# Splitting the sparse-attention weights in the first feed-forward layer and keeping both parts in DRAM

## The chip, the cores and the metric

One core of a Trainium2 chip runs the whole program in one launch. The metric is the device time in microseconds (us) of that launch; lower is better. The engines that matter are TensorE (PE, matrix products), VectorE (DVE), ScalarE (ACT), GpSimd (POOL) and the DMA queues that SyncE (SP) and GpSimd issue to. Data lives in DRAM, in SBUF (128 partitions) and in PSUM, into which PE writes.

## The reference, cut to what matters

Two layers over T = 1040 tokens (16 learned ones, then 1024), D = 1024. Layer 0 mixes tokens with gated linear attention (GLA), layer 1 with sparse attention (DSA); a SwiGLU feed-forward layer follows each.

```python
def dsa_mixer(h, w_in, g_kv, w_uk, w_uv, w_out, rel_bias):
    proj = h @ w_in
    q, c, q_idx, k_idx, w_idx = jnp.split(proj, [s1, s2, s3, s4], axis=-1)
    c = rmsnorm(c, g_kv)
...
        s_idx = jnp.einsum('bqhd,bsd->bqhs', qib, k_idx) * IDX_DIM ** -0.5
        score = jnp.einsum('bqhs,bqh->bqs', jax.nn.relu(s_idx), wb)
        top_val, top_idx = lax.top_k(score, n_sel)          # 256 keys of each query
        c_sel = jax.vmap(lambda cb, ib: cb[ib])(c, top_idx)
        q_lat = jnp.einsum('bqhd,hcd->bqhc', qb, w_uk)
        logits = jnp.einsum('bqhc,bqkc->bhqk', q_lat, c_sel) * ATT_HEAD_DIM ** -0.5
        logits = logits + bias                               # T5 relative bias, then softmax
        u = jnp.einsum('bhqk,bqkc->bqhc', p, c_sel)
        return jnp.einsum('bqhc,hcd->bqhd', u, w_uv)
    return o @ w_out

def swiglu(h, w_in, w_out):
    gate, up = jnp.split(h @ w_in, 2, axis=-1)
    return (jax.nn.silu(gate) * up) @ w_out
```

Everything is float32.

## The kernel before

**Arithmetic.** Each float32 operand of a product is split into two parts of the type fp32r, a rounded high part (`wh`, `xh`, ...) and the rest (`wl`, `xl`, ...). `mm3` then makes each product with three matmuls: high by high (L198), high by low (L199) and low by high (L200). So every weight that arrives from DRAM has to be split before PE can use it.

**Weights.** `Weights` holds the list of all weight tiles in their order of use. `get` hands out a tile and, with `ahead`, starts the load of the next one. `load_split` loads a tile of 128 x 2048 (1 MB; 128 x 1024 for some) in two pieces into raw buffers (`wraw`, two of them, SP's queue, L184), makes the high part with a cast (L186 on ACT, or L188 on GpSimd where `whigh` is set) and the low part with a subtraction (L189, on the engine `wlow`). The parts go to a ring of two slots, each a pair `wh`, `wl`. `wlow` is VectorE, except from the index stage to the end of attention, where it is GpSimd; `whigh` is GpSimd during the top-k stage.

**Stages in time.** GLA runs to about 400 us and its output projection to 450. The first feed-forward layer runs from 450 to about 1290: eleven groups of two gate tiles, and in each group per gate tile (`hidden`) three pieces of the token axis (352, 344, 344 columns), with the down projection of the group before in between. Then come the index stage with its scores (`kidx`, `qidx0`, `qidx1`; to about 1381), the top-k stage (to about 1605), attention (to about 1810), the output projection (`do0` to `do3`, to about 1880) and the second feed-forward layer to the end. In the top-k stage the program's text interleaves two kinds of steps: a step-by-step search on VectorE for each query's threshold (L1053 counts with `jd`; L1062 `below`, L1070 `cand`, L1073 and L1076 `flip` move the bounds, on 128 x 3 or 128 x 4 numbers), and the units of latent, queries (`dq0` to `dq3`), keys and values (`ukv0`) on PE with their evictions. Attention splits the other three `ukv` tiles in pieces of 512 columns.

**Order.** Each engine takes its instructions in the program's order, SP and GpSimd also their DMA issues, and each instruction waits for its own inputs and for free buffers. Buffers come from pools: a tile of a name with n buffers waits for the release of the one n before it.

Of the kernel before, what the change touches and what calls it, by code (L numbers as in the profile page):

```python
# [9 lines left out]
F32 = mybir.dt.float32  # L10
F32R = mybir.dt.float32r
# [22 lines left out]
WIDE = [(META, 512), (META + 512, 512)]  # L34
REL = 1
RING, RAW = 2112, 1056
EARLY = 5
GROUPS = (([7, 1, 4, 3], (2, 2)), ([5, 2, 6], (1, 1)))
N1, S2, M2, S3, M3 = 1, 3, 2, 8, 2
# [40 lines left out]
class Weights:  # L80
# [4 lines left out]

    def load(self, i):
        if i < len(self.seq) and self.seq[i] is not None and i not in self.tiles:
            _, src, n = self.seq[i]
            self.tiles[i] = self.k.load_split(src, n)

    def get(self, name, ahead=True):
        i = self.i
# [16 lines left out]
class Trunk:  # L109
    def __init__(self, ctx, tc, io, out):  # L110
        self.tc, self.nc, self.io, self.out = tc, tc.nc, io, out
        nc = self.nc
        self.main = ctx.enter_context(tc.tile_pool(name="main", bufs=1))
        self.ring = ctx.enter_context(tc.tile_pool(name="ring", bufs=2))
        self.rawp = ctx.enter_context(tc.tile_pool(name="raw", bufs=2))
        self.psp = ctx.enter_context(tc.tile_pool(name="ps", bufs=8, space=bass.MemoryType.PSUM))
        m = self.main
        self.later = Later()
        self.wlow = nc.vector
        self.whigh = None  # L120
        self.xh = m.tile([128, KT, T], F32R, name="xh")
        self.xl = m.tile([128, KT, T], F32R, name="xl")

        self.xm = m.tile([128, KT, 48], F32R, name="xm")
        self.h = m.tile([128, KT, T], F32, name="h0", tag="H")

        self.ident = m.tile([128, 128], F32, name="ident")
        self.mean = m.tile([128, 128], F32, name="mean")
        self.sufm = m.tile([128, 128], F32R, name="sufm")
        self.totm = m.tile([128, 2], F32, name="totm")  # L130
        self.gains = m.tile([128, 6, KT], F32, name="gains")
        self.eps = m.tile([128, 1], F32, name="eps")
        nc.vector.memset(self.mean, 1.0 / D)
        nc.vector.memset(self.eps, EPS)
        nc.gpsimd.tensor_scalar_mul(self.xm[:, :, META:32], self.mean.rearrange("p (k c) -> p k c", k=KT), 0.0)

        nc.scalar.activation(m.tile([128, 1], F32, name="root"), self.eps, AF.Sqrt)
        self.sufraw = m.tile([128, 128], F32, name="sufraw")

        seq = [("ka%d" % i, io["w_ka"][i], KT * 264) for i in range(2)]  # L140
        for h in range(4):
            seq += [("gq%d" % h, io["w_gq"][h], 1024), ("gr%d" % h, io["w_gr"][h], 2048),
                    ("gv%d" % h, io["w_gv"][h], 2048)]
        seq += [("go%d" % i, io["w_go"][i], 2048) for i in range(4)]
        seq += self.ffn_seq(0)
        seq += [("kidx", io["w_kidx"], 1024)]
        seq += [("qidx%d" % i, io["w_qidx"][i], 2048) for i in range(2)]
        seq += [("c", io["w_c"], 2048)]
        seq += [("dq%d" % i, io["w_dq"][i], 2048) for i in range(4)]
        seq += [None]  # L150
        seq += [("do%d" % i, io["w_do"][i], 2048) for i in range(4)]
        seq += self.ffn_seq(1)
        self.w = Weights(self, seq)

        dram = lambda name, shape: nc.dram_tensor(name, shape, F32).ap()
        self.s_h = dram("s_h", (128, KT, T))
        self.s_rel = dram("s_rel", (8, NREL))
        self.s_skew = dram("s_skew", (8, 128, NREL))
# [14 lines left out]
    def ps(self, dt=F32):  # L173
        return self.psp.tile([128, 512], dt, name="ps")

    def load_split(self, src, n, pool=None, tags=("wh", "wl"), cap=RING, raw=None, piece=RAW):
        nc = self.nc
        pool = pool or self.ring
        hi = pool.tile([128, cap], F32R, name=tags[0])
        lo = pool.tile([128, cap], F32R, name=tags[1])  # L180
        for a in range(0, n, piece):
            e = min(n, a + piece)
            r = raw() if raw else self.rawp.tile([128, RAW], F32, name="wraw")
            nc.sync.dma_start(r[:, : e - a], src[:, a:e])  # L184
            if self.whigh is None:
                nc.scalar.copy(hi[:, a:e], r[:, : e - a])  # L186
            else:
                self.whigh.tensor_copy(hi[:, a:e], r[:, : e - a])  # L188
            self.wlow.tensor_sub(lo[:, a:e], r[:, : e - a], hi[:, a:e].bitcast(F32))  # L189
        return hi, lo  # L190

    def split(self, hi, lo, src, low=None):
        self.nc.scalar.copy(hi, src)  # L193
# [466 lines left out]
            after(c)  # L660


    def ffn(self, pool, tmp, chunks, last_chunks, squares, after):
        nc, w, later = self.nc, self.w, self.later
        v = nc.vector
        G = NF // 2

        def hidden(hh, hl, wi, q, a, n):
            pg = self.proj_fm(wi, 256, 0, a, n)
            later.tick()  # L670
            pu = self.proj_fm(wi, 256, 128, a, n)
            sg = tmp.tile([128, 512], F32, name="sg")
            t = tmp.tile([128, 512], F32, name="t")
            nc.scalar.activation(sg[:, :n], pg[:, :n], AF.Silu)  # L674
            v.tensor_mul(t[:, :n], sg[:, :n], pu[:, :n])  # L675
            self.split(hh[:, q, a : a + n], hl[:, q, a : a + n], t[:, :n])
            later.tick()
# [17 lines left out]
        for g in range(G):  # L695
# [39 lines left out]
            else:  # L735
                chunks = WIDE if self.layer else chunks
                for q in range(2):
                    wi = w.get("fi%d" % (2 * g + q))
                    for a, n in chunks:
                        hidden(hh, hl, wi, q, a, n)  # L740
                    if q == 0 or g == G - 2:
                        wo = w.get("fo%d" % (g - 1 + q))
                        order = [(d, c) for d in range(KT) for c in chunks]
                        if q:
                            order = [(d, c) for c in chunks for d in range(KT)]
                        for d, (a, n) in order:
                            out(*(prev if q == 0 else (hh, hl)), wo, d, a, n)
                        later.tick()
            prev = (hh, hl)

    def ffn_phase(self, layer, begun, norm_row, last_chunks, after, emit=None, cover=()):

# [2 lines left out]
        with ExitStack() as ctx:  # L755
# [33 lines left out]

            applies = []  # L790
            self.out_end(begun, lambda c: squares(*chunks[c]), normed)
            self.ffn(pool, tmp, chunks, last_chunks, squares, ended)
            for f in cover[:1]:
                f()
            self.later.drain()
# [4 lines left out]
    def index_begin(self):  # L800

        self.begun = {}

        def keys(c):
            a, n = ALL[c]
            self.begun["k", a] = self.proj_fm(self.wk, 128, 0, a, n)

        def first():
            self.wlow = self.nc.gpsimd
            self.wk = self.w.get("kidx")  # L810
            keys(0)

        def rest():
            keys(1)
            self.wq0 = self.w.get("qidx0", ahead=False)
            for e in range(2):
                self.begun["q", 144, e] = self.proj_fm(self.wq0, 256, e * 128, 144, 384)

        return first, rest

    def dsa(self):
# [1 line left out]
        v = nc.vector  # L823
        off = [sum(nkeys(j) for j in range(b)) for b in range(9)]
        with ExitStack() as ctx:
            self.wlow = nc.gpsimd
            self.kv = {}
            dp = ctx.enter_context(tc.tile_pool(name="dsa", bufs=1))
            cth = dp.tile([128, 2, T], F32R, name="cth")
# [75 lines left out]
            with tc.tile_pool(name="topk", bufs=1) as tp, tc.tile_pool(name="cn", bufs=2) as cp:  # L905
                qf = self.main.tile([128, 8, SEQ], F32, name="qf", tag="H")
                steps = self.topk(tp, sc, mask, off)
                costs = [1.7] * 66 + [MASK] * 8
                self.whigh = nc.gpsimd

                def parts(c, j):

                    a, n = FRAMES[c]
# [29 lines left out]
                        done += 1  # L943
                later.drain()
                att.begin(steps, len(costs) - done)
                self.whigh = None
            att.run(ctx, mp)
            h = self.main.tile([128, KT, T], F32, name="h1", tag="H")
            for k in range(KT):
# [224 lines left out]
            v.memset(mask[0:64, off[b + 1] - 64 : off[b + 1]], NEG)  # L1174
            yield

    def keys(self, pool, p, raw=None, piece=RAW):

        kh = self.ring.tile([128, RING], F32R, name="wh")
        kl = self.ring.tile([128, RING], F32R, name="wl")  # L1180
        uh, ul = self.load_split(self.io["w_ukv"][p], 1024, pool, ("uh", "ul"), 1024, raw, piece)
        self.kv[p] = (uh, ul, kh, kl)
        for e in range(2):
            for a, n in ALL:
                q = self.ps()[:, :n]
                for j in range(2):
                    s = slice((e * 2 + j) * 128, (e * 2 + j) * 128 + 128)
                    self.mm3(q, uh[:, s], ul[:, s], self.cth[:, j, a : a + n], self.ctl[:, j, a : a + n],
                             j == 0, j == 1)
                s = slice(e * T + a, e * T + a + n)  # L1190
                self.split(kh[:, s], kl[:, s], q)
# [26 lines left out]
    def attention(self, sp, mask, off, sc):  # L1218
# [128 lines left out]
        def run(ctx, mp):  # L1347
# [7 lines left out]
            for j, (hd, m) in enumerate(units):  # L1355
# [18 lines left out]
                if m == 3 and hd < 6:  # L1374
                    table(hd + 2)
                if m == KEYS_AT and hd % 2 and hd < 7:
                    self.keys(mp, hd // 2 + 1, lambda: ap.tile([128, 512], F32, name="uraw"), 512)
                if m == 0 and hd == 7:
                    self.wlow = v
                    w.past_stop()  # L1380

        buf = SimpleNamespace(begin=begin, run=run)
# [94 lines left out]
```

## Time and profile before

| | |
|---|---|
| time, median of 3 runs | 2663.42 us (2662.87 to 2664.26) |
| profiled execution, its own time | 2667.23 us |
| its span | 2665.0 us |
| PE, DVE, ACT, POOL busy | 2530.1, 1417.1, 965.7, 255.2 us |
| PE's share of the span | 95% |
| mean granted clock of PE | 0.975 |

The span is what the profiler saw of the program; the profiled execution's own time is 2.2 us more. Busy shares are means over very different stages: in the feed-forward layers PE has no idle time, in the stages between them other engines end the waits.

### The profile page before, as it was taken

The numbers are of one execution on the slowest core, as the hardware profiler recorded it, in microseconds if no ns is written. First come the engines' busy times: TensorE is split into PE (matmuls) and PEld (weight loads), VectorE is DVE, ScalarE is ACT, GpSimd is POOL, SyncE is SP. The second block draws the span as 40 slices with busy tenths as digits, with TensorE's granted clock in tenths as the row PEclk, the third lists the DMA queues.
The fourth block names the chain that finished last, engine by engine and source line by source line (L and its number), as shares of the span: only waits on it lengthen the run. The fifth ranks groups of instructions, "written<-read, shape, count | busy, mean of one in ns | idle before, by whom it ended". The sixth has DMA issues, their size and how long they took to land.

```text
span 2665.0 us, 37404 instructions
## 1 busy us (share of the span) xinstructions
PE 2530.1 (95%) x15072; PEld 2342.3 (88%) x15072; DVE 1417.1 (53%) x3196; ACT 965.7 (36%) x1981; POOL 255.2 (10%) x222
## 2 busy tenths in 40 slices
PE   7999999999999999999898749999999999999997
PEld 6899999999999999999778739999988888888887
DVE  7565565643333333345699997673633333333346
ACT  5654452521111111114475667772511111111114
POOL 3000000200000000001212125540200000000001
PEclk9899999999999999999998969999999999999999
DMA  3113113011111111112100001012011111111111
GB/s 116 40 35 105 39 38 108 32 53 43 48 48 48 48 48 48 48 56 91 39 17 33 25 1 41 25 45 107 32 48 48 48 48 48 48 48 48 48 48 64
DMA packets 45168, 133.32 MB, mean 50 GB/s; under 512 B 4442, under 2 KB 15986, under 8 KB 44995
## 3 DMA queue, kind: packets, MB, share of 16 engines
q1 hardware_dynamic: 43634, 125.99, 14.0%
q0 software_dynamic: 1360, 4.95, 0.7%
q8 instruction: 118, 1.93, 0.3%
q14 instruction: 56, 0.45, 0.1%
HBM read 122.43 MB, written 13.27 MB: 51 GB/s over the span
## 4 chain that ended last, share of the span: by engine, by line
PE 79%; DVE 12%; issue 4%; ACT 3%; POOL 1%; DMA 0%; SPq 0%; ACTq 0%; DVEq 0%; POOLq 0%
PE ps L198 25%; PE ps L200 25%; PE ps L199 25%; DVE jd L1053 4%; PE ps L1282 1%; DVE sc L877 1%; POOL xl L194 1%; PE ps L499 1%; DVE no L304 1%; DVE xl L194 0%; DVE flip L1073 0%; PE ps L218 0%; PE ps L1294 0%; ACT L292 0%; DVE na L267 0%
## 5 line engine op out<-in xcount | busy, mean ns | idle before, releaser
L198 PE MATMUL ps<-xh,wh 128*128 128x344 f32 (+6 forms) x2808 | 951.0, 339 | 21.8 <-ACT qf L1000 12.3
L200 PE MATMUL ps<-xh,wl 128*128 128x344 f32 (+6 forms) x2808 | 944.2, 336 | 3.5 <-DVE wl L189 3.1
L199 PE MATMUL ps<-xl,wh 128*128 128x344 f32 (+6 forms) x2808 | 946.1, 337 | 1.3 <-POOL xl L194 0.9
L198 PEld LDWEIGHTS ps<-xh,wh 128*128 128x128 f32 x2808 | 532.2, 190 | 55.9 <-ACT qf L1000 14.7
L199 PEld LDWEIGHTS ps<-xl,wh 128*128 128x128 f32 x2808 | 532.5, 190 | 31.2 <-POOL xl L194 1.8
L200 PEld LDWEIGHTS ps<-xh,wl 128*128 128x128 f32 x2808 | 532.5, 190 | 30.6 <-DVE wl L189 3.3
L675 DVE TENSOR_TENSOR t<-sg,ps 128x344 f32<-128x344 f32 (+4 forms) x116 | 65.1, 561 | 653.5 <-PE ps L200 652.6
L186 ACT CAST wh<-wraw 128x1056 fp32r<-128x1056 f32 (+2 forms) x175 | 179.4, 1049 | 593.4 <-PE ps L199 588.3
L688 DVE TENSOR_TENSOR h<-h,ps 128x344 f32<-128x344 f32 (+3 forms) x456 | 251.3, 567 | 168.0 <-PE ps L200 167.9
L198 PE MATMUL ps<-hh,wh 128*128 128x512 f32 (+2 forms) x800 | 280.3, 350 | 0.0
L199 PE MATMUL ps<-hl,wh 128*128 128x512 f32 (+2 forms) x800 | 280.0, 350 | 0.0
L200 PE MATMUL ps<-hh,wl 128*128 128x512 f32 (+2 forms) x800 | 279.8, 350 | 0.0
L189 DVE TENSOR_TENSOR wl<-wraw,wh 128x1056 fp32r<-128x1056 f32 (+2 forms) x167 | 201.8, 1230 | 78.0 <-ACT wh L186 77.0
L198 PE MATMUL ps<-wh,xh 128*128 128x256 f32 (+9 forms) x560 | 174.8, 312 | 16.1 <-ACT xh L193 6.9
L200 PE MATMUL ps<-wh,xl 128*128 128x256 f32 (+9 forms) x560 | 168.7, 301 | 3.6 <-POOL xl L194 1.6
L194 POOL TENSOR_TENSOR xl<-no,xh 128x344 fp32r<-128x344 f32 (+5 forms) x52 | 59.5, 1150 | 1164.6 <-ACT xh L193 1164.5
L674 ACT ACTIVATE sg<-ps 128x344 f32<-128x344 f32 (+4 forms) x116 | 57.8, 498 | 304.0 <-PE ps L200 303.9
L199 PE MATMUL ps<-wl,xh 128*128 128x256 f32 (+9 forms) x560 | 167.2, 299 | 0.0
L193 ACT CAST hh<-t 128x344 fp32r<-128x344 f32 (+4 forms) x116 | 60.0, 517 | 285.0 <-DVE t L675 285.0
L198 PEld LDWEIGHTS ps<-hh,wh 128*128 128x128 f32 x800 | 150.0, 188 | 14.6
L199 PEld LDWEIGHTS ps<-hl,wh 128*128 128x128 f32 x800 | 150.3, 188 | 14.3
L200 PEld LDWEIGHTS ps<-hh,wl 128*128 128x128 f32 x800 | 150.5, 188 | 13.9
(283 smaller groups left out, 3376.4 us busy)
## 6 DMA issues: line engine op xcount, KB each, us to landing
wraw<-in_w_fi SPq DMA_DIRECT2D x44, 528.0 KB, 3.7
wraw<-in_w_fi SPq DMA_DIRECT2D x44, 496.0 KB, 4.8
wraw<-in_w_fo SPq DMA_DIRECT2D x22, 528.0 KB, 3.8
wraw<-in_w_fo SPq DMA_DIRECT2D x22, 496.0 KB, 4.8
s_skew<-s_rel POOLq DMA_DIRECT2D x8, 583.5 KB, 12.5
h<-in_ht SPq DMA_DIRECT2D x8, 520.0 KB, 5.5
wraw<-s_skew SPq DMA_DIRECT2D x8, 520.0 KB, 3.4
h<-s_h SPq DMA_DIRECT2D x8, 512.0 KB, 6.1
```

Of the source, the lines that this page charges most:

```text
L186: nc.scalar.copy(hi[:, a:e], r[:, : e - a])
L189: self.wlow.tensor_sub(lo[:, a:e], r[:, : e - a], hi[:, a:e].bitcast(F32))
L193: self.nc.scalar.copy(hi, src)
L194: (low or self.nc.vector).tensor_sub(lo, src, hi.bitcast(F32))
L198: mm(p, sh, mh, start=first, stop=False, skip_group_check=True)
L199: mm(p, sh, ml, start=False, stop=False, skip_group_check=True)
L200: mm(p, sl, mh, start=False, stop=last, skip_group_check=True)
L304: v.scalar_tensor_tensor(o, x, self.gains[:, row, k : k + 1], y, op0=OP.mult, op1=OP.mult)
L674: nc.scalar.activation(sg[:, :n], pg[:, :n], AF.Silu)
L675: v.tensor_mul(t[:, :n], sg[:, :n], pu[:, :n])
L688: v.tensor_add(self.h[:, d, a : a + n], self.h[:, d, a : a + n], p[:, :n])
L1053: v.tensor_scalar(j[:, : nkeys(b)], src(b), cand, None, op0=op, op1=OP.add, accum_out=out)
```

## The change

The weights `kidx`, `qidx`, `c`, `dq`, `ukv` and `do` are no longer split where they are used. A new generator, `split_early`, cuts them into 54 pieces of 128 x 512. In the nine middle groups of the first feed-forward layer each call of `hidden` (54 in all) is followed by one step of it: SP loads the piece into a buffer of the ring `sg` (three, shared with the layer's own `sg`), GpSimd casts it to `eh` and subtracts to `el`, and SP stores both to DRAM tensors (`s_kidx_h`, `s_kidx_l` and so on). Later `load_parts` fills a ring slot with two DMAs on GpSimd's queue, high part and low part, straight into `wh` and `wl`. The first feed-forward layer's buffer `t` has 352 columns in place of 512. The switches `whigh` and the parameters `raw` and `piece` go; `wlow` is VectorE throughout.

```diff
     def load(self, i):
         if i < len(self.seq) and self.seq[i] is not None and i not in self.tiles:
-            _, src, n = self.seq[i]
-            self.tiles[i] = self.k.load_split(src, n)
+            name, src, n = self.seq[i]
+            self.tiles[i] = self.k.load_parts(name, n) if src is None else self.k.load_split(src, n)
...
+        self.parts = {name: [nc.dram_tensor("s_%s_%s" % (name, x), (128, n), F32).ap() for x in "hl"]
+                      for name, _, n in self.early}
...
+    def load_parts(self, name, n, pool=None, tags=("wh", "wl"), cap=RING):
+
+        pool = pool or self.ring
+        ts = [pool.tile([128, cap], F32R, name=t) for t in tags]
+        for t, src in zip(ts, self.parts[name]):
+            self.nc.gpsimd.dma_start(t[:, :n], src)
+        return tuple(ts)
+
+    def split_early(self, pool, raw):
+
+        nc = self.nc
+        for name, src, n in self.early:
+            for a in range(0, n, PRE):
+                e = min(n, a + PRE)
+                r = raw()[:, : e - a]
+                hi = pool.tile([128, PRE], F32R, name="eh")[:, : e - a]
+                lo = pool.tile([128, PRE], F32R, name="el")[:, : e - a]
+                nc.sync.dma_start(r, src[:, a:e])
+                nc.gpsimd.tensor_copy(hi, r)
+                nc.gpsimd.tensor_sub(lo, r, hi.bitcast(F32))
+                for p, t in zip(self.parts[name], (hi, lo)):
+                    nc.sync.dma_start(p[:, a:e], t.bitcast(F32))
+                yield
...
-            t = tmp.tile([128, 512], F32, name="t")
+            t = tmp.tile([128, 512 if self.layer else 352], F32, name="t")
...
                     for a, n in chunks:
                         hidden(hh, hl, wi, q, a, n)
+                        next(beside, None)
...
-            self.wlow = self.nc.gpsimd
             self.wk = self.w.get("kidx")
...
-            self.wlow = nc.gpsimd
...
-                self.whigh = nc.gpsimd
-
...
-                self.whigh = None
...
-        uh, ul = self.load_split(self.io["w_ukv"][p], 1024, pool, ("uh", "ul"), 1024, raw, piece)
+        uh, ul = self.load_parts("ukv%d" % p, 1024, pool, ("uh", "ul"), 1024)
```

On GpSimd, before, from the last part of the index stage's input (`xl<-no,xh`) through the splits of `qidx1`, `c` and `dq0` to the casts of `dq1`:

```order
L194 TENSOR_TENSOR xl<-no,xh 128x344
L189 TENSOR_TENSOR wl<-wraw,wh 128x1056
L189 TENSOR_TENSOR wl<-wraw,wh 128x992
L189 TENSOR_TENSOR wl<-wraw,wh 128x1056
L189 TENSOR_TENSOR wl<-wraw,wh 128x992
L188 CAST wh<-wraw 128x1056
L188 CAST wh<-wraw 128x992
L189 TENSOR_TENSOR wl<-wraw,wh 128x1056
L189 TENSOR_TENSOR wl<-wraw,wh 128x992
L188 CAST wh<-wraw 128x1056
L188 CAST wh<-wraw 128x992
```

The same place of the changed program, where `L200` is `load_parts` (the rows name the weight, not its number):

```order
L221 TENSOR_TENSOR xl<-no,xh 128x344
L200 DMA wh<-s_qidx_h 128x2048
L200 DMA wl<-s_qidx_l 128x2048
L200 DMA wh<-s_c_h 128x2048
L200 DMA wl<-s_c_l 128x2048
L200 DMA wh<-s_dq_h 128x2048
L200 DMA wl<-s_dq_l 128x2048
L200 DMA uh<-s_ukv_h 128x1024
L200 DMA ul<-s_ukv_l 128x1024
L1266 TENSOR_TENSOR sc<-wraw,mask 128x144
L200 DMA wl<-s_dq_l 128x2048
```

GpSimd's casts and subtractions are gone there, and DMA issues stand in their place; one bias addition of attention (`sc<-wraw,mask`) now stands ahead of the load of `dq1`.

On SP, before, in the middle of the first feed-forward layer (weights `fi` of the gate and up projection, `fo` of the down projection):

```order
L184 DMA wraw<-in_w_fi 128x1056
L184 DMA wraw<-in_w_fi 128x992
L184 DMA wraw<-in_w_fi 128x1056
L184 DMA wraw<-in_w_fi 128x992
L184 DMA wraw<-in_w_fo 128x1056
L184 DMA wraw<-in_w_fo 128x992
```

The same place of the changed program:

```order
L190 DMA wraw<-in_w_fi 128x1056
L190 DMA wraw<-in_w_fi 128x992
L212 DMA sg<-in_w_kidx 128x512
L216 DMA s_kidx_h<-eh 128x512
L216 DMA s_kidx_l<-el 128x512
L212 DMA sg<-in_w_kidx 128x512
L216 DMA s_kidx_h<-eh 128x512
L216 DMA s_kidx_l<-el 128x512
L212 DMA sg<-in_w_qidx 128x512
L216 DMA s_qidx_h<-eh 128x512
L216 DMA s_qidx_l<-el 128x512
L190 DMA wraw<-in_w_fi 128x1056
```

Nine DMAs, a load and two stores for each of three pieces, now stand between the loads of one weight tile and those of the next.

## Rows read from the trace of the kernel before

**Rows 1.** The page, chain of work that ended last, by engine.

```profile
PE 79%; DVE 12%; issue 4%; ACT 3%; POOL 1%; DMA 0%; SPq 0%; ACTq 0%; DVEq 0%; POOLq 0%
```

**Rows 2.** Windows: us, busy time and instructions per engine, granted clock, DMA.

```profile
core 0: us, PE busy (x) PEld busy (x) DVE busy (x) ACT busy (x) POOL busy (x), PEclk, DMA share, GB/s
600.00:800.00 200.00, 200.00 (x1265) 200.00 (x1265) 72.00 (x123) 31.94 (x51) 0.00 (x0) 1.00 0.14 46
...
1400.00:1450.00 50.00, 42.24 (x257) 41.93 (x258) 49.59 (x177) 23.82 (x64) 13.43 (x8) 0.86 0.10 34
1450.00:1500.00 50.00, 44.34 (x261) 43.03 (x259) 48.56 (x147) 27.82 (x57) 10.62 (x7) 0.93 0.13 41
1500.00:1550.00 50.00, 24.84 (x133) 22.73 (x134) 48.34 (x165) 36.38 (x79) 2.37 (x1) 0.80 0.00 1
1550.00:1600.00 50.00, 27.34 (x116) 22.60 (x116) 49.25 (x142) 30.72 (x72) 14.68 (x9) 0.67 0.00 1
```

**Rows 3.** Timeline of GpSimd: start, us, instruction, count, idle before and its releaser.

```profile
1287.04 0.57 POOL L834 DMA_DIRECT2D gkv<-in_gkv  x1 [1.20 <-ACT xh L193]
...
1293.26 4.71 POOL L189 TENSOR_TENSOR wl<-wraw,wh 128x1056 fp32r<-128x1056 f32 x2 [4.69 <-ACT wh L186]
...
1410.10 2.03 POOL L188 CAST wh<-wraw 128x1056 fp32r<-128x1056 f32 x2 [67.75 <-PE ps L200]
1412.09 4.69 POOL L189 TENSOR_TENSOR wl<-wraw,wh 128x1056 fp32r<-128x1056 f32 x2
1441.80 2.03 POOL L188 CAST wh<-wraw 128x1056 fp32r<-128x1056 f32 x2 [25.02 <-PE ps L199]
...
1464.32 2.03 POOL L188 CAST wh<-wraw 128x1056 fp32r<-128x1056 f32 x2 [15.77 <-PE ps L199]
...
1473.73 2.41 POOL L189 TENSOR_TENSOR ul<-wraw,uh 128x1024 fp32r<-128x1024 f32 x1
...
1609.92 1.28 POOL L189 TENSOR_TENSOR ul<-uraw,uh 128x512 fp32r<-128x512 f32 x1
```

**Rows 4.** Timeline of VectorE in the top-k stage.

```profile
1410.73 0.46 DVE L1062 TENSOR_TENSOR below<-cnt,thr 128x4 int32<-128x4 f32 x1
...
1412.17 2.38 DVE L1073 SCALAR_TENSOR_TENSOR flip<-pos,cand 128x4 int32<-128x4 int32 x1
...
1451.80 0.16 DVE L1073 SCALAR_TENSOR_TENSOR flip<-pos,cand 128x4 int32<-128x4 int32 x1
...
1473.90 2.26 DVE L1073 SCALAR_TENSOR_TENSOR flip<-pos,cand 128x4 int32<-128x4 int32 x1
```

**Rows 5.** Timeline of VectorE in the scores of the index stage.

```profile
1329.77 1.05 DVE L877 SCALAR_TENSOR_TENSOR sc<-rt,wx,sc 128x272 f32<-128x272 f32 x2
...
1336.62 3.58 DVE L877 SCALAR_TENSOR_TENSOR sc<-rt,wx,sc 128x272 f32<-128x272 f32 x2
```

**Rows 6.** Timeline of TensorE: index stage, scores, attention.

```profile
1288.89 0.32 PE L200 MATMUL ps<-xh,wl 128*128 128x344 f32 x1
...
1295.77 0.69 PE L200 MATMUL ps<-xh,wl 128*128 128x384 f32 x1 [0.46 <-POOL wl L189]
...
1340.74 0.42 PE L868 MATMUL ps<-kxh,qx 128*128 128x328 f32 x1 [2.05 <-ACT rt L872]
...
1343.19 0.64 PE L868 MATMUL ps<-kxh,qx 128*128 128x328 f32 x1 [1.57 <-ACT rt L872]
...
1797.21 0.38 PE L1306 MATMUL ps<-big 80*128 80x256 f32 x1 [1.08 <-DVE big L1274]
```

**Rows 7.** Timeline of ScalarE in the output projection, around the split of `do3`.

```profile
1854.00 2.00 ACT L186 CAST wh<-wraw 128x1056 fp32r<-128x1056 f32 x2 [6.21 <-PE ps L199]
```

**Rows 8.** The page, DMA issues: count, KB each, median us from issue to landing.

```profile
s_skew<-s_rel POOLq DMA_DIRECT2D x8, 583.5 KB, 12.5
...
h<-s_h SPq DMA_DIRECT2D x8, 512.0 KB, 6.1
```

**Rows 9.** The tile `s_skew`: its issues, ns min/median/max, first and last start.

```profile
L604 POOL DMA_DIRECT2D s_skew<-s_rel x8: 515/517/552, 227.0 to 230.6; - x8
```

**Rows 10.** The tile `s_h`: its issues.

```profile
L950 SPq DMA_DIRECT2D h<-s_h x8: 326/439/601, 1809.1 to 1812.5; - x8
```

More of the change, by code (lines that the diff above doesn't have):

```diff
@@ L36 @@
 RING, RAW = 2112, 1056
+PRE = 512
 EARLY = 5
@@ L145, in __init__ @@
         seq += self.ffn_seq(0)
[L146 to L149, printed above, removed]
+        self.early = [("kidx", io["w_kidx"], 1024)]
+        self.early += [("qidx%d" % i, io["w_qidx"][i], 2048) for i in range(2)]
+        self.early += [("c", io["w_c"], 2048)]
+        self.early += [("dq%d" % i, io["w_dq"][i], 2048) for i in range(4)]
+        self.early += [("ukv%d" % i, io["w_ukv"][i], 1024) for i in range(4)]
+        self.early += [("do%d" % i, io["w_do"][i], 2048) for i in range(4)]
+        self.parts = {name: [nc.dram_tensor("s_%s_%s" % (name, x), (128, n), F32).ap() for x in "hl"]
+                      for name, _, n in self.early}
+        seq += [(name, None, n) for name, _, n in self.early[:8]]
         seq += [None]
-        seq += [("do%d" % i, io["w_do"][i], 2048) for i in range(4)]
+        seq += [(name, None, n) for name, _, n in self.early[12:]]
         seq += self.ffn_seq(1)
@@ L174, in ps, with load_split @@
         return self.psp.tile([128, 512], dt, name="ps")
-    def load_split(self, src, n, pool=None, tags=("wh", "wl"), cap=RING, raw=None, piece=RAW):
+    def load_split(self, src, n, pool=None, tags=("wh", "wl"), cap=RING):
         nc = self.nc
@@ L180, in load_split @@
         lo = pool.tile([128, cap], F32R, name=tags[1])
-        for a in range(0, n, piece):
-            e = min(n, a + piece)
-            r = raw() if raw else self.rawp.tile([128, RAW], F32, name="wraw")
+        for a in range(0, n, RAW):
+            e = min(n, a + RAW)
+            r = self.rawp.tile([128, RAW], F32, name="wraw")
             nc.sync.dma_start(r[:, : e - a], src[:, a:e])
[L185 to L188, printed above, removed]
+            nc.scalar.copy(hi[:, a:e], r[:, : e - a])
             self.wlow.tensor_sub(lo[:, a:e], r[:, : e - a], hi[:, a:e].bitcast(F32))
         return hi, lo
+    def load_parts(self, name, n, pool=None, tags=("wh", "wl"), cap=RING):
[18 more added lines that the diff above has]
+                yield
     def split(self, hi, lo, src, low=None):
@@ L660, in out_end, with ffn @@
             after(c)
-    def ffn(self, pool, tmp, chunks, last_chunks, squares, after):
+    def ffn(self, pool, tmp, chunks, last_chunks, squares, after, beside):
         nc, w, later = self.nc, self.w, self.later
@@ L749, in ffn @@
             prev = (hh, hl)
+            if g == G - 2:
+                for _ in beside:
+                    pass
     def ffn_phase(self, layer, begun, norm_row, last_chunks, after, emit=None, cover=()):
@@ L791, in ffn_phase @@
             self.out_end(begun, lambda c: squares(*chunks[c]), normed)
-            self.ffn(pool, tmp, chunks, last_chunks, squares, ended)
+            beside = iter(())
+            if layer == 0:
+                beside = self.split_early(ctx.enter_context(self.tc.tile_pool(name="early", bufs=1)),
+                                          lambda: tmp.tile([128, 512], F32, name="sg"))
+            self.ffn(pool, tmp, chunks, last_chunks, squares, ended, beside)
             for f in cover[:1]:
@@ L945, in dsa @@
                 att.begin(steps, len(costs) - done)
-                self.whigh = None
             att.run(ctx, mp)
@@ L1175, in topk, with keys @@
             yield
-    def keys(self, pool, p, raw=None, piece=RAW):
+    def keys(self, pool, p):
         kh = self.ring.tile([128, RING], F32R, name="wh")
         kl = self.ring.tile([128, RING], F32R, name="wl")
-        uh, ul = self.load_split(self.io["w_ukv"][p], 1024, pool, ("uh", "ul"), 1024, raw, piece)
+        uh, ul = self.load_parts("ukv%d" % p, 1024, pool, ("uh", "ul"), 1024)
         self.kv[p] = (uh, ul, kh, kl)
@@ L1376, in run @@
                 if m == KEYS_AT and hd % 2 and hd < 7:
-                    self.keys(mp, hd // 2 + 1, lambda: ap.tile([128, 512], F32, name="uraw"), 512)
+                    self.keys(mp, hd // 2 + 1)
                 if m == 0 and hd == 7:
-                    self.wlow = v
                     w.past_stop()
```

## The prediction, on record before the result

> **What bounds the kernel now.** I read the chain of waits first, then busy times in stretches, then the timelines of the stretches that the change touches. The chain says that PE ends 79% of the span and VectorE 12% [rows 1]. The stretches say where: in the first feed-forward layer PE is busy all of 200 us and VectorE 72, GpSimd not at all; from 1400 to 1600 it is the other way round, VectorE is busy 48 to 50 of every 50 us and PE 25 to 44 [rows 2]. So a microsecond of VectorE's time counts in the top-k stage, and GpSimd's time is free in the feed-forward layer as long as nothing waits for it. A change of this kernel under 0.2% (5.3 us) can't be told from none.
>
> In the top-k stage GpSimd splits `dq0` to `dq3` and `ukv0`: 2.0 us of casts and 4.7 of subtractions for each `dq` [rows 3]. VectorE isn't waiting for their results there; it is slowed by their running. `flip` (L1073, both inputs in SBUF, 128 x 4 numbers) takes 0.16 us at 1451.80 and 2.38 at 1412.17, 0.1 us after a GpSimd subtraction began [rows 3, 4]. Its end is that of the subtraction's first half. This is the cost the change can take away.
>
> **What it removes.**
> *Top-k.* Between 1410.73 and 1473.90 I count 14 small VectorE instructions (`below`, `cand`, `flip`) that lie beside such a split and are longer than the same instruction elsewhere; rows 4 show the first, the costliest, a normal one and the last. Their excess, duration less 0.155 to 0.16 us each: 4.3 us at `dq1`, 5.3 at `dq2`, 4.6 at `dq3`, 2.7 at `ukv0`, together 16.9. VectorE is the bound there [rows 2], so I count all of it.
> *Scores.* The split of `dq0` falls on the end of the scores: two `sc` take 3.58 us where two take 1.05 [rows 5]. Earlier scores are slowed as well, but PE has no gap behind them; the two gaps that it has are 2.05 and 1.57 us [rows 6]. Gain 3.6.
> *Attention and output.* PE waits 1.08 us for `big`, which stood behind VectorE's split of `do` [rows 6]. Gain 1.1. The 1.28 us subtractions of `ukv1` to `ukv3` [rows 3] go too; PE uses these tiles some 20 us later, so nothing ends on them. ACT's casts go; it isn't the bound: 0.
> Sum of the gains: 21.6.
>
> **What it adds, in the first feed-forward layer.** A piece costs GpSimd a cast of 512 columns (a quarter of the 2.03 us for 2048, 0.5) and a subtraction (1.28, the same shape at 1609.92) [rows 3]: 1.8 us per gate tile. A gate tile is 48 matmuls, at 1265 in 200 us [rows 2] 7.6 us, so GpSimd keeps pace. A subtraction may hold up a VectorE instruction by up to 1.28 us; VectorE idles 64% there [rows 2], and what PE waits for there (`t`, from a PSUM bank, and the parts of `hh`, read only by the next group's down projection) has spare banks and a gate tile's time. SP now has nine DMAs between weight loads. The third load waits for a buffer until about two gate tiles are through (15.2 us); with a landing of 6.1 us at most (eight larger loads at once took that [rows 8]) and 1.8 of GpSimd its stores go out by 23.1 us, about at the weight change at 3 x 7.6 = 22.8, when the next weight's load goes out anyway; that one has the 22.8 us of the following weight to arrive. I count 0. Without that cover each piece could cost its 1.28 us: 54 x 1.28 = 69.
>
> **What it adds, later: 2 MB per weight on GpSimd's queue.** Each part is 1 MB and both must cross, where before 1 MB was already waiting in the raw buffers. No row shows a DMA of GpSimd's queue that turns f32 into fp32r, so I bound it. Slow end: the eight `s_skew` transfers of that queue (DRAM to DRAM) have a median of 12.5 us to landing, with about 1.8 us of issues before the middle one [rows 8, 9]: half of 4.78 MB in 14.3, so 2.1 MB in 12.6. Fast end: the eight `h` loads of SP's queue (DRAM to SBUF) have 6.1, with 1.7 of issues ahead [rows 8, 10]: 2.1 MB in 7.8. The route is that of the second, the queue that of the first; I take 9.4, a third of the way from the fast end.
>
> The cover of each load is the time from the slot's release to its first use:
> - `qidx1`: `kidx` is done at 1289.2 and PE took `qidx1`'s low part at 1295.8, after 0.46 us of wait [rows 6]. Cover 6.6, loss 2.8 (1.2 to 6.0). Before, the raw data was there, and a split of 4.71 us followed [rows 3].
> - `do3`: its slot is free at 1854.0 [rows 7] and it is needed two output units later, 48 matmuls or 7.6 us [rows 2]. Loss 1.8 (0.2 to 5.0).
> - `dq1`, `dq2`, `dq3`: slots come free at 1410.1, 1441.8 and 1464.3 [rows 3], and each weight is needed when the one before it is done, the next such time: cover 31.7 and 22.5, or 27 and 17 once the splits' 4 to 5 us are gone. Hidden; `kidx`, `qidx0`, `c`, `dq0`, `do2` and the `ukv` too.
>
> GpSimd's issues stand in its order; `gkv`'s took 0.57 us [rows 3]. Ahead of `dq1` stands one `sc` of attention, whose inputs are ready before 1410. Nothing else queues behind a waiting issue at a point where it ends a wait.
>
> Here a rule of the Trainium skill speaks against the change. Rows 9 show eight issues of GpSimd's queue at 0.52 to 0.55 us, none of them held up, but not beside a VectorE that is busy without a break. The Trainium skill (SBUF — State Buffer, Who interferes with whom) says that a DMA issued from GpSimd has its descriptors written by GpSimd, which can't do so while VectorE runs an instruction in a mode that takes both ports, so that the transfer starves. No run here shows that; it is the first rival. Of the size, the Trainium skill (DMA: Bandwidth & Descriptors, Anatomy of one DMA) gives 2.0 us plus a microsecond for each 436 KB; by that I estimate 4.4 us for one part and 6.8 for two that follow each other, a loss of 0.2 in all and a time of 2642.
>
> **Sum.** −21.6 + 2.8 + 1.8 = −17.0 us. The profiled execution took 2667.2, so 2650.2 for one like it; the median is 3.8 below the profiled one: 2646.4.
>
> **Rivals.**
> 1. *The loads are late* (slower). If a weight of two parts takes t, the loss at `qidx1` and `do3` is (t − 6.6) + (t − 7.6); it eats the 21.6 at t = 17.9 us, 1.4 times the slow end. At twice the fast end, 15.6, it is 17.0, and the time 2659; at 1.5 times the slow end, 18.9, it is 23.5 and the time 2665; at twice the slow end, 25.2, it is 36.2 and the time 2678. Speaks for it: a busy VectorE and a conversion in the transfer that no row shows. Against: VectorE is not fully busy at `qidx1`, and the queue's eight issues were even. Chance 0.13, spread over 2655 to 2678.
> 2. *PE takes over part of the gain.* Where the splits lie, PE is idle only 7.8 us (1400 to 1450) and 5.7 (1450 to 1500) [rows 2]; the gains there are 4.3 + 5.3 and 4.6 + 2.7. If PE had to do its work within these stretches, 1.8 + 1.6 are lost: 2650. Against: from 1500 to 1600 PE idles 48 of 100 us and VectorE 2, so VectorE's queue would catch up. Chance 0.15.
> 3. *The feed-forward layer is disturbed* (slower): GpSimd's subtraction delays `t` or `hh`, or SP's in-order waits delay a weight. It decides from 17.0 / 54 = 0.31 us per gate tile; at 0.5 us it is 27 us and the time 2673. For it: PE has no idle time there. Against: the slack above. Chance 0.10.
> 4. *More gain*: fast DMAs (no loss) give 2642, and a PE clock that now stands at 0.80 to 0.93 from 1450 to 1550 [rows 2] may rise with fewer stops. 2634 to 2641, chance 0.07.
> That the change does not do what it says, I exclude: the order of GpSimd's instructions shows the splits gone from there.
>
> **How the numbers follow.** The forecast, 2641 to 2651, has 0.55. Faster by over 0.2% means below 2658.1: the forecast, rivals 2 and 4 (0.77, less 0.03 for case 2 going deeper) and a little of rival 1: 0.76. Slower means above 2668.7: most of rival 3 and the upper third of rival 1: 0.14. Same, the rest: 0.10. The range 2638 to 2661 leaves out most of rival 3, the upper half of rival 1 and the lowest of rival 4, about 0.2.
>
> **What would show it.** Right: GpSimd idle in the top-k stage but for DMA issues and the `xl` and `sc` that stay; no `flip` above 0.3 us between 1400 and 1480 except beside those; the stage some 17 us shorter; a PE gap of 2 to 4 us at `qidx1`'s low part, released by a DMA, and one of about 2 us at `do3`; PE at 200 of 200 in the first feed-forward layer. Wrong: PE gaps in the feed-forward layer in each gate tile; PE gaps of 10 us and more at `qidx1` or `do3`; landings over 18 us; or VectorE's instructions as long as before beside DMA issues of GpSimd.

## The result and the profile after

The changed kernel took 2636.73 us (median of 4 runs, 2635.26 to 2637.91) against 2663.74 of the kernel before on the same chip (4 runs): a ratio of 0.9899, 95% interval 0.9882 to 0.9916, so 27.0 us faster. The direction was forecast; the size was not: 2646.4 was predicted, and the time lies 1.3 us below the range (2638 to 2661). The profiled execution after took 2636.64 us, as its median; that of before stood 3.8 above the median quoted there, so the traces differ by 30.5 us where the runs differ by 27.0.

The windows of after, the same columns as [rows 2], with the end of the first feed-forward layer added. The changed top-k stage begins some 7 us earlier, so its windows are shifted, by 10 us.

```profile
600.00:800.00 200.00, 200.00 (x1266) 200.00 (x1265) 76.03 (x124) 32.21 (x52) 35.45 (x36) 1.00 0.35 116
...
1390.00:1440.00 50.00, 43.27 (x283) 42.56 (x282) 49.44 (x217) 30.16 (x81) 2.59 (x5) 0.97 0.23 85
1440.00:1490.00 50.00, 46.82 (x296) 45.97 (x294) 48.36 (x172) 34.11 (x71) 1.05 (x2) 1.00 0.12 43
1490.00:1540.00 50.00, 20.23 (x101) 18.38 (x102) 48.55 (x152) 34.72 (x74) 4.71 (x2) 0.73 0.00 0
```

In the first feed-forward layer GpSimd is now busy 35 of 200 us, VectorE 4 us more than in [rows 2], the DMA engines carry 116 GB/s in place of 46, and PE still has no idle time. In the top-k stage GpSimd has gone from 13.4 and 10.6 us per window to 2.6 and 1.1. VectorE is as busy as before, but gets through more: PE's instructions in the two windows are 283 and 296 where they were 257 and 261.

GpSimd's timeline of after in that stage, to set against [rows 3]:

```profile
1395.12 0.45 POOL L1266 TENSOR_TENSOR sc<-wraw,mask 128x144 f32<-128x144 f32 x1 [18.88 <-DVE mask L1189]
1404.85 0.54 POOL L200 DMA_DIRECT2D wl<-s_dq_l  x1 [9.28 <-PE ps L227]
1405.39 0.55 POOL L200 DMA_DIRECT2D wh<-s_dq_h  x1
1430.05 0.53 POOL L200 DMA_DIRECT2D wh<-s_dq_h  x1 [24.10 <-PE ps L227]
1430.56 0.54 POOL L200 DMA_DIRECT2D wl<-s_dq_l  x1
1452.56 0.53 POOL L200 DMA_DIRECT2D wh<-s_dq_h  x1 [21.46 <-PE ps L227]
```

Two issues of half a microsecond stand where 6.7 us of casts and subtractions stood. VectorE beside the first pair, to set against [rows 4]:

```profile
1404.53 0.16 DVE L1093 TENSOR_TENSOR below<-cnt,thr 128x4 int32<-128x4 f32 x1
1404.72 0.16 DVE L1101 SCALAR_TENSOR_TENSOR cand<-below,flip 128x4 int32<-128x4 int32 x1
...
1404.92 0.16 DVE L1104 SCALAR_TENSOR_TENSOR flip<-pos,cand 128x4 int32<-128x4 int32 x1
...
1406.15 0.16 DVE L1107 TENSOR_SCALAR flip<-flip 128x4 int32<-128x4 int32 x1
```

All are at 0.16 us: an issue on GpSimd's queue does not slow them, nor do the transfers.

The loads themselves. TensorE at `qidx1`, to set against [rows 6], and the tile `s_dq_l` (low parts of `dq0` to `dq3`) with its time from issue to landing:

```profile
1292.51 0.69 PE L225 MATMUL ps<-xh,wh 128*128 128x384 f32 x1 [0.34 <-DMA wh<-s_qidx_h]
```

```profile
L200 POOL DMA_DIRECT2D wl<-s_dq_l x4: 535/536/543, 1333.1 to 1453.1; - x4
...
DMA to landing us min/median/max: 5.8/7.1/7.7
```

PE waits 0.34 us for `qidx1`. The first part lands about 5 us after its issue (5.0 at `qidx1` and at `do3`), the second about 7 us after its own, so both parts, issued half a microsecond apart, are there after some 7.5 us. The gap at `qidx1` is a wait for the high part. At `do3` PE has no gap.

**Where the 30.5 us of the traces lie.** PE runs the same 15,072 matmuls in nearly the same order in every kernel here. I compared the start of the matmul of the same count, counted from the beginning, at the ends of the stages, in the trace of before and of after:

| from, to (start after, us) | before loses to after |
|---|---|
| start to 1215, nearly the end of the first feed-forward layer | 0.4 |
| to 1241, its end | 1.8 |
| to 1335, index stage and most scores | 0.6 |
| to 1347, end of the scores | 3.6 |
| to 1551, top-k stage | 17.3 |
| to 1776, attention | 5.7 |
| to the last matmul | 0.7 |

The remaining 0.4 lie behind the last matmul. Read at 1580 in place of 1551, the top-k stage has 16.9 and attention 6.1, so these figures hold to some 0.3 us. The two large parts were in the sum. The 1.8 and most of the 5.7 were not, and the loss that I had entered for loads is missing.

### The profile page after: what moved, and what is told of

The parts are those of the page before. It is cut to its first block, busy times and chain, and to the rows that moved or that the text cites. A ratio compares the mean times of both kernels' runs of the same rounds, so it can differ in the third digit from the quotient of the medians.

```text
span 2634.5 us, 37837 instructions
## 1 busy us (share of the span) xinstructions
PE 2518.2 (96%) x15072; PEld 2333.1 (89%) x15072; DVE 1390.8 (53%) x3187; ACT 949.9 (36%) x1960; POOL 325.0 (12%) x332
## 4 chain that ended last, share of the span: by engine, by line
PE 39%; DVE 9%; issue 1%; ACT 1%; POOL 0%; DMA 0%; ACTq 0%; DVEq 0%; POOLq 0%
PE ps L226 12%; PE ps L227 12%; PE ps L225 12%; DVE jd L1084 4%; PE ps L1313 1%; DVE sc L911 1%; PE ps L1325 1%; PE ps L902 0%; POOL xl L221 0%; ACT rt L906 0%; DVE pre L1199 0%; PE ps L904 0%; PE ps L1301 0%; DVE h L331 0%; DVE xl L221 0%
## 5 line engine op out<-in xcount | busy, mean ns | idle before, releaser
L191 ACT CAST wh<-wraw 128x1056 fp32r<-128x1056 f32 (+2 forms) x160 | 163.9, 1049 | 581.5 <-PE ps L226 558.8
L192 DVE TENSOR_TENSOR wl<-wraw,wh 128x1056 fp32r<-128x1056 f32 (+2 forms) x158 | 193.0, 1244 | 73.7 <-ACT wh L191 72.4
L225 PEld LDWEIGHTS ps<-wh,xh 128*128 128x128 f32 x560 | 109.6, 196 | 23.1 <-ACT xh L220 7.2
## 6 DMA issues: line engine op xcount, KB each, us to landing
s_skew<-s_rel POOLq DMA_DIRECT2D x8, 583.5 KB, 14.1
```

The source lines that it names most:

```text
L225: mm(p, sh, mh, start=first, stop=False, skip_group_check=True)
```

## The experiments

Times are medians; ratios are to the kernel before on the same chip, with 95% intervals. The runs of the kernel before beside them had medians from 2663.9 to 2667.2, so ratios are compared, not times. The changed kernel, run again beside three of these, gave 0.9898 (0.9884 to 0.9911), 2636.19 us:

> The changed kernel again, beside the three others on the same chip, so that differences of 2 us can be read against it: a ratio of 0.990 to the kernel before.

**Theory 1:** GpSimd's casts and subtractions hold up VectorE while they run, whoever needs their results. **Theory 2:** what was saved is a wait for split weights or an emptier ScalarE. Further open were the price of the loads, and what the parts outside the top-k stage contribute.

**Old split for `dq` and `ukv0` alone** (`load_old` is the text of the old `load_split`):

```diff
-            self.tiles[i] = self.k.load_parts(name, n) if src is None else self.k.load_split(src, n)
+            k, g = self.k, self.k.nc.gpsimd
+            how = {'dq': (1, 1)}.get(name.rstrip("0123")) if src is None else None
+            if how:
+                src = [s for m, s, _ in k.early if m == name][0]
+                self.tiles[i] = k.load_old(src, n, high=g if how[0] else None, low=g if how[1] else None)
...
+            uh, ul = self.load_old(self.io["w_ukv"][p], 1024, pool, ("uh", "ul"), 1024, high=g, low=g)
```

> The changed kernel, but dq0 to dq3 and ukv0 are loaded raw and split on GpSimd in their old places (their early pieces are still made and stored, and not used). Theory 1, GpSimd's splits hold up VectorE: the top-k stage gives back 16.9 us and the end of the scores 3.6, so 2636.7 + 20.5 = 2657 us. Theory 2, the gain comes from elsewhere (an emptier ScalarE, weights that arrive earlier): little of it is undone, under 2645 us.

2655.75 us, 0.9964 (0.9952 to 0.9977): 17.3 us slower than the changed kernel by the ratios. By the matmul count it loses 3.6 at the end of the scores and 16.4 from there to the end of the top-k stage, as theory 1 had it (and 2.0 at the very start, where both kernels have the same code). Theory 2 falls as far as these weights go.

**The same GpSimd work, read by nobody.** After each load of a `dq` and of `ukv0`, GpSimd casts and subtracts its columns into a scratch tile:

```diff
+        if name[:2] == "dq" or name == "ukv0":
+            g = self.nc.gpsimd
+            for a in range(0, n, 640):
+                e = min(n, a + 640)
+                r = ts[0][:, a:e].bitcast(F32)
+                q = self.dumb.tile([128, 640], F32R, name="dumb")[:, : e - a]
+                g.tensor_copy(q, r)
+                g.tensor_sub(q, r, q.bitcast(F32))
```

> The changed kernel, and in the top-k stage GpSimd also casts and subtracts the columns of each dq and of ukv0, as the old split did, into a scratch tile that nobody reads. Theory 1 (it is GpSimd's running that costs, not a wait for its results): four dq at 4.3 to 5.3 us and ukv0 at 2.7 give about 21.5 us, so 2658 us, with flip and below of 1 to 2 us beside these splits. Theory 2 (VectorE or PE waited for the results of the split): nobody waits, 2637 us.

2654.50 us, 0.9961 (0.9947 to 0.9974): 16.5 us slower, and 18.0 by the matmul count, all of it in the top-k stage. GpSimd's timeline, and below it VectorE's, beside one of these splits:

```profile
1444.36 1.56 POOL L208 TENSOR_TENSOR dumb<-wh,dumb 128x640 fp32r<-128x640 f32 x1
1445.98 0.74 POOL L207 CAST dumb<-wh 128x640 fp32r<-128x640 f32 x1
1446.80 1.58 POOL L208 TENSOR_TENSOR dumb<-wh,dumb 128x640 fp32r<-128x640 f32 x1
1448.45 0.72 POOL L207 CAST dumb<-wh 128x640 fp32r<-128x640 f32 x1
1449.25 1.57 POOL L208 TENSOR_TENSOR dumb<-wh,dumb 128x640 fp32r<-128x640 f32 x1
```

```profile
1444.57 1.37 DVE L1102 TENSOR_TENSOR below<-cnt,thr 128x4 int32<-128x4 f32 x1
...
1446.17 0.57 DVE L1113 SCALAR_TENSOR_TENSOR flip<-pos,cand 128x4 int32<-128x4 int32 x1
1446.66 0.88 DVE L1093 TENSOR_SCALAR_CACHE_REDUCE jd<-mask,cand 128x656 bf16<-128x656 bf16 x1
...
1447.48 0.93 DVE L1116 TENSOR_SCALAR flip<-flip 128x4 int32<-128x4 int32 x1
...
1449.41 1.43 DVE L1113 SCALAR_TENSOR_TENSOR flip<-pos,cand 128x3 int32<-128x3 int32 x1
```

`below` ends at 1445.94, as the subtraction that began at 1444.36 does (1445.92); `flip` at 1449.41 ends at 1450.84, the subtraction at 1450.82. Each holds until the GpSimd instruction is through. The long `jd` at 1446.66 runs beside a subtraction at its usual 0.88. So it is the running that costs, and it costs some of VectorE's instructions and not others. It came to less than the 21.5 expected of four `dq`; whether the smaller pieces met more of `jd` I did not separate.

**VectorE splits for itself**, in the kernel before:

```diff
-                self.whigh = nc.gpsimd
+                self.wlow = nc.vector
```

> The kernel before, but dq0 to dq3 and ukv0 are split by ScalarE (high part) and VectorE itself (low part, 1.2 us per half) in place of GpSimd. VectorE, which bounds that stage, gets 10.9 us more work of its own. Theory 1: it no longer stands still for 20.5 us beside GpSimd, so it is 9.6 us faster all the same: 2654 us. Theory 2 (GpSimd took work off VectorE without a cost): 10.9 us slower, 2674 us.

2651.24 us, 0.9947 (0.9933 to 0.9960): 14.1 us faster than before, with more work on the engine that bounds the stage. That is 4.5 more than expected. By the matmul count 2.2 come at the end of the scores and 7.6 in the top-k stage (16.9 less some 8.5 of its own subtractions would be 8.4): together 9.8, where 9.6 were expected. The rest lies behind it, 3.3 in attention and 2.1 after it. The edit reaches that far: `wlow` stays VectorE to the end of attention, so the low parts of `ukv1` to `ukv3` (six subtractions of 0.7 to 1.2 us) leave GpSimd too, which the expectation does not say.

**Without the early split.** Both parts of each later weight come from the weight itself and nothing is split in the first feed-forward layer:

```diff
-        for t, src in zip(ts, self.parts[name]):
+        src = [s for m, s, _ in self.early if m == name][0]
+        for t in ts:
...
-                beside = self.split_early(ctx.enter_context(self.tc.tile_pool(name="early", bufs=1)),
-                                          lambda: tmp.tile([128, 512], F32, name="sg"))
+                pass
```

> The changed kernel without the early split: nothing is loaded, split or stored in the first feed-forward layer, and both parts of each later weight are loaded from the weight itself, so the low part is wrong and the output is not the reference's. The price of the early split by the prediction: none, 2636.7 us. Rival: it costs some of the gain, at 0.1 us per piece 5.4 us, so 2631 us.

2636.76 us, 0.9891 (0.9877 to 0.9904). The matmul count differs from after by at most 0.1 us at every stage. The early split costs nothing that these runs show.

**Twice the bytes at `qidx1` and `do3`:**

```diff
-            self.nc.gpsimd.dma_start(t[:, :n], src)
+            for _ in range(2 if name in ("qidx1", "do3") else 1):
+                self.nc.gpsimd.dma_start(t[:, :n], src)
```

> The changed kernel, with each part of qidx1 and do3 loaded twice, 4 MB instead of 2 for each, about 15 us instead of 7.5. If the covers that I read (6.6 and 7.6 us) are right, the loads now end 8 us late at qidx1 and 7 at do3: 2651 us. If something else covers them: under 2642 us.

2646.61 us, 0.9926 (0.9914 to 0.9939): 7.2 us slower by the ratios, 10.0 by the matmul count (5.8 at `qidx1`, 4.2 at `do3`). The doubled loads took 13 us, not 15. GpSimd's and then TensorE's timeline of this kernel:

```profile
1286.19 0.54 POOL L201 DMA_DIRECT2D wh<-s_qidx_h  x1 [0.78 <-PE ps L228]
...
1291.54 0.53 POOL L201 DMA_DIRECT2D wh<-s_qidx_h  x1 [4.26 <-DMA wh<-s_qidx_h]
```

```profile
1296.65 0.69 PE L226 MATMUL ps<-xh,wh 128*128 128x384 f32 x1 [5.72 <-DMA wh<-s_qidx_h]
```

```profile
1840.13 0.40 PE L226 MATMUL ps<-xh,wh 128*128 128x344 f32 x1 [3.23 <-DMA wh<-s_do_h]
...
1842.63 0.43 PE L228 MATMUL ps<-xh,wl 128*128 128x344 f32 x1 [0.69 <-DMA wl<-s_do_l]
```

The waits are 5.7 and 3.9 us; with covers of 6.6 and 7.6, 13 us would give 6.4 and 5.4. But the longer waits are for the high parts. The second load of a part was issued only when the first had landed, so a high part was there some 10.5 us after its first issue, and the low one after 13. PE was ready for the high part 4.7 us after the issue at `qidx1` and 7.4 at `do3`. So a load half a dozen microseconds longer does cost, and the cover of 6.6 that I read at `qidx1` is not that of the high part, which is 2 us shorter. In the changed kernel the high part, after 5 us, is hardly late for it.

**The parts outside the top-k stage, one by one.** `ukv1` to `ukv3`, `do`, and `kidx`, `qidx`, `c` were each put back to the old split by the same edit as `dq` above (`do` and `kidx` with the low part on VectorE, the others on GpSimd).

> The changed kernel, but ukv1 to ukv3 are loaded raw and split in pieces of 512 columns in attention, as before. By the prediction nothing ends on them: 2636.7 us. By the gaps of TensorE in attention in the trace of before (0.73, 1.07 and 0.33 us ended by ptl, beside those splits): 2 us, so 2639 us.

> The changed kernel, but do0 to do3 are loaded raw and split on ScalarE and VectorE, as before. By the prediction 1.1 us in attention come back and 1.8 us of waiting for do3's load go: 2636 us. If the load of do3 is hidden, as the trace of after has it (two parts landed after 7.5 us, 7.6 us of cover): 1.1 to 1.5 us slower, 2638 us.

> The changed kernel, but kidx, qidx0, qidx1 and c are loaded raw and split as before (kidx on VectorE, the others' low parts on GpSimd). By the prediction the wait for qidx1's load, 2.8 us, goes: 2634 us. By the trace of after (a wait of 0.34 us for that load, and 2 us gained at the end of the first feed-forward layer, where VectorE no longer splits kidx): about 2 us slower, 2639 us.

They gave 0.9903 (0.9889 to 0.9917), 0.9902 (0.9888 to 0.9915) and 0.9901 (0.9887 to 0.9914): each slower by a few ten-thousandths, which the time alone can't tell from no change. The matmul counts do place something: 2.7 us in attention with the old `do`, 1.8 at the end of the first feed-forward layer with the old `kidx`, and with the old `ukv` 2.4 in attention, of which 1.3 came back after it. So all three went into one kernel, only `dq` and `ukv0` loaded as parts:

> The changed kernel with only dq0 to dq3 and ukv0 loaded as parts; kidx, qidx, c, ukv1 to ukv3 and do are split in their old places and ways. By the prediction's terms (no waits of 4.6 us for the loads of qidx1 and do3, 1.1 us in attention back): 3.5 us faster than the changed kernel, a ratio of 0.9886 to the kernel before. By the three single runs (each some 2 us slower than the changed kernel, near the limit of what the time can tell): 5 to 7 us slower than the changed kernel, 0.992.

2644.07 us, 0.9922 (0.9910 to 0.9935): 6.4 us slower than the changed kernel run beside it by the ratios, 7.9 by the times. By the count it loses 1.8 at the end of the first feed-forward layer and 4.9 in attention. My own terms would have made it 3.5 faster. This is the run that refutes them.

**What the old `ukv` cost.** The waits of ScalarE in attention, in the kernel before (what waits, for what; us in total, times, longest):

```profile
ACT sc L1258 <- DVE sm L1250: 12.1, 15, 1.4
ACT xh L193 <- DVE gkv L1314: 8.0, 17, 0.8
ACT uh L186 <- DMA uraw<-in_w_ukv: 4.1, 3, 2.3
```

ScalarE, which evicts `big` for PE, stood 4.1 us for raw pieces: there was one buffer `uraw`, so the second half of a tile could only be loaded when GpSimd was through with the first, and the cast of that half waited in ScalarE's queue in front of everything else. In the run with the old `ukv` ScalarE waits there too, 2.9 us in all:

```profile
ACT uh L214 <- DMA uraw<-in_w_ukv: 2.9, 2, 1.5
```

One of its waits, with ScalarE's cast of `big` behind it and VectorE's subtraction, which stood idle for that cast:

```profile
1644.88 0.62 ACT L214 CAST uh<-uraw 128x512 fp32r<-128x512 f32 x1 [1.37 <-DMA uraw<-in_w_ukv]
...
1645.67 0.74 ACT L1324 CAST big<-ps 16x256 fp32r<-16x256 f32 x2
```

```profile
1646.44 0.41 DVE L1325 TENSOR_TENSOR big<-ps,big 16x256 fp32r<-16x256 f32 x1 [1.99 <-ACT big L1324]
```

Behind these two waits TensorE has its gaps:

```profile
1648.70 0.38 PE L1357 MATMUL ps<-big 80*128 80x256 f32 x1 [0.70 <-DVE ptl L238]
...
1703.43 0.39 PE L1357 MATMUL ps<-big 80*128 80x256 f32 x1 [0.89 <-DVE ptl L238]
```

With two buffers of half the width, against the run with the old `ukv`:

```diff
-            uh, ul = self.load_old(self.io["w_ukv"][p], 1024, pool, ("uh", "ul"), 1024, raw, 512, low=self.nc.gpsimd)
+            uh, ul = self.load_old(self.io["w_ukv"][p], 1024, pool, ("uh", "ul"), 1024, raw, 256, low=self.nc.gpsimd)
...
-                    self.keys(mp, hd // 2 + 1, lambda: ap.tile([128, 512], F32, name="uraw"))
+                    self.keys(mp, hd // 2 + 1, lambda: ap.tile([128, 256], F32, name="uraw", bufs=2))
```

> As the run with ukv1 to ukv3 in the old way, but with two raw buffers of 256 columns instead of one of 512, in the same memory. If ScalarE lost its time there by standing for a raw load in its queue (4.1 us in three waits in the trace of before), these waits go, and with them the gaps of TensorE of 0.70 and 0.89 us: 2637 us, that of the changed kernel. If the casts themselves cost it, the gaps stay: 2639 us.

2637.61 us, 0.9900 (0.9886 to 0.9913). The wait of the same place:

```profile
ACT uh L214 <- DMA uraw<-in_w_ukv: 2.2, 4, 0.8
```

Its longest is 0.8 in place of 1.5, its sum 2.2 in place of 2.9, and PE's gaps of 0.70 and 0.89 us there are gone. By the time this can't be told from one buffer or from the changed kernel. By the matmul count it loses 1.1 us in attention where one buffer lost 2.4, so about half of the loss went with the long waits. The pieces were halved as well (a cast lasts 0.41 in place of 0.62 us, a subtraction on GpSimd 0.73 in place of 1.28), which this run does not separate. The kernel in which VectorE splits for itself helps: it keeps ScalarE's casts of 512 columns and the one buffer, but its ScalarE waits 0.5 us there in place of 4.1, and by the count it gains 1.1 and 2.1 us at the two places where the changed kernel gains 1.1 and 2.1. So it is not the casts themselves that cost.

**GpSimd's last splits to VectorE**, in the changed kernel:

```diff
-QPOOL, KEYS0, PC = (1,), 0, 1.0
+QPOOL, KEYS0, PC = (), 0, 1.0
```

> The changed kernel, and the three splits xl<-qf that GpSimd still makes in the top-k stage go to VectorE. It gets 3 x 1.23 = 3.7 us more work and loses 5.1 us of standing still beside GpSimd (below, xl and y at 1520, 1534 and 1547 us): 1.4 us faster, 2635 us. If handing work to GpSimd pays there: 3.7 us slower.

2635.06 us, 0.9888 (0.9873 to 0.9904), beside 0.9898 of the changed kernel. The six `xl<-qf` take 1.18 to 1.23 us each, and none stands any more, but the difference of 1.1 us is within the uncertainty and the traces agree to 0.1 at the end. A version clearly better than the changed kernel was not found.

## Why the prediction was wrong in size, point by point

| term | predicted | by the runs |
|---|---|---|
| top-k stage | −16.9 | −17.3 (undone: +16.4) |
| end of the scores | −3.6 | −3.6 (undone: +3.6) |
| early split, first feed-forward layer | 0 | 0.0 |
| `kidx` no longer split at its end | not in the sum | −1.8 (undone: +1.8) |
| load of `qidx1` | +2.8 | about 0 |
| attention, `ukv` and `do` | −1.1 | −5.7 (undone: +4.9) |
| load of `do3` | +1.8 | 0 |
| sum | −17.0 | −27.0 of the runs |

The figures of the last column are those of the matmul count, whose whole is 30.5 because the profiled execution of before was slow by 3.5; where these lie in its trace no run shows. The terms that were undone add up to 26.7.

- *What bounds, and the mechanism: right.* The 14 instructions counted one by one gave 16.9, and the stage gave 17.3 back. Scratch splits that nobody reads cost 16.5 to 18 us there. Rival 2 falls with it: PE took none of that gain.
- *The first feed-forward layer: right.* GpSimd's groups between 500 and 1240 us after (what, shapes, count; busy, mean ns; idle before) show the pieces at 2.0 us each, a little above my 1.8. They make VectorE's 200 us there 4 us busier, and hold up PE nowhere that shows. Rival 3 falls.

```profile
L214 POOL TENSOR_TENSOR el<-sg,eh 128x512 fp32r<-128x512 f32 x54 | 71.6, 1327 | 4.3
L213 POOL CAST eh<-sg 128x512 fp32r<-128x512 f32 x54 | 35.6, 658 | 525.6 <-DMA sg<-in_w_dq 156.5 <-DMA sg<-in_w_do 154.8 <-DMA sg<-in_w_qidx 92.4
```

- *The step that failed first: "I take 9.4, a third of the way from the fast end".* The transfers took 7.5 us for 2.1 MB, just under the fast end of 7.8. The cast in the transfer and the queue cost nothing that shows. With 7.5 in place of 9.4 my own covers give 0.9 and 0 in place of 2.8 and 1.8; 0.3 and 0 were measured. That is 4 of the 10 us. I had also taken the two parts as one that lands whole, against the cover of the low part; at `qidx1` it is the high part that PE wants first, and that one lands after 5 us. Rival 1 falls. VectorE was busy 49.4 of 50 us when `dq1` and `dq2` were loaded, and their low parts landed within the 5.8 to 7.7 us of all four. So the starving of descriptors that the Trainium skill (SBUF — State Buffer, Who interferes with whom) warns of did not show here; whether any of VectorE's instructions beside these loads ran in the mode that it speaks of, the trace does not say. The estimate of 6.8 us for two parts by the Trainium skill (DMA: Bandwidth & Descriptors, Anatomy of one DMA) is 0.7 below what was measured, nearer than mine.
- *The second: "ACT's casts go; it isn't the bound: 0", and "PE uses these tiles some 20 us later, so nothing ends on them".* I asked who waits for the result of the split, and not who stands behind it in the queue. ScalarE's cast waited there for a DMA, and `big` behind it, which PE wants at once. By the count the old `ukv` lost 2.4 us in attention by itself. The old `do` lost 2.7, where I had listed one gap of 1.1: a further 1.3 lie at an earlier subtraction for `do` on VectorE (at 1772.57 in the trace of before), which I did not list. Attention gave 5.7 in place of 1.1, some 4.6 us of the 10.
- *The third: `kidx`.* Its split on VectorE at the end of the first feed-forward layer was nowhere in the list of what is removed. It stood in VectorE's queue ahead of the additions to `h` that PE's next step waits for: 1.8 us. VectorE and TensorE in the kernel before, where this gap is; in the changed kernel it is not there, and with the old `kidx` it is back, at 1.6 us:

```profile
1236.10 1.22 DVE L189 TENSOR_TENSOR wl<-wraw,wh 128x1024 fp32r<-128x1024 f32 x1
```

```profile
1243.00 0.42 PE L198 MATMUL ps<-xh,wh 128*128 128x344 f32 x1 [1.57 <-DVE h L688]
```

- *The range.* Rival 4 had the fast loads at 2642 and a little more for the clock; the two omissions went the same way, and no case held them. That the time lies within rival 4's 2634 to 2641 is luck: the granted clock rose in two windows (0.86 and 0.93 to 0.97 and 1.00) and fell in the next (0.80 to 0.73), and the terms that were undone account for the gain without it.

Open: why the old `ukv` lost 2.4 us in attention, where its gaps are 0.70 and 0.89, and got 1.3 back after it; what was gained 2.1 us after attention when VectorE split for itself; and whether the last `xl<-qf` splits are better on VectorE.

## What to carry to other kernels

Before giving an engine work because it idles, look at what another engine's instructions last while it works: here an idle GpSimd took work off a VectorE that bounded the stage and cost it more than the work itself, and moving that work to a stage where VectorE had slack was free. For a removed instruction ask both questions, who waits for its result and who stands behind it in its queue while it waits for its own input. Where a new transfer replaces a split, take the cover from slot release to first use, for each part by itself, and expect a loss only for what exceeds it.

## What the hardware showed that I had not expected

- A DMA of GpSimd's queue that turns f32 in DRAM into fp32r in SBUF lands 1 MB in about 5 us and a second, issued half a microsecond later, at about 7.5 us, beside a VectorE busy 49.4 of 50 us as well as at `do3`. By the prediction's working 2.1 MB of `s_skew` on the same queue, DRAM to DRAM, took 12.6, two thirds longer [rows 8, 9].
- An issue on that queue (0.53 to 0.55 us) did not lengthen VectorE's small instructions (0.16 us), while a cast or subtraction did, until its end.
- Kernels with the same code up to there differ by up to 2 us at the 960th matmul (168 us), in both directions, so that single traces are to be compared from a stage's start to its end and not by their spans.
